# A decoder block in split fp32 on one core: SBUF pools in another order, so that weights start at a multiple of 128 bytes and the other large tiles 64 bytes past one

## The chip, the core and the metric

One core of a Trainium2 chip. The metric is device time in microseconds, from the start to the end of one execution. Two things beside it come from the profile of one execution: its span (first to last recorded instruction), and the start and duration of every instruction on the engines TensorE (PE; its weight loads are listed apart as PEld), VectorE (DVE), ScalarE (ACT), GpSimd (POOL) and of the DMAs that SyncE (SP) and GpSimd issue.

## The reference

One decoder layer on x of 512 tokens by 2048 channels, in float32:

```
h = rmsnorm(x);  proj = h @ w_in            # 2048 x 5132, three head groups
mixed = concat(pool_mixer, gated_deltanet, rglru_mixer)
x = x + mixed @ w_out                       # 2048 x 2048
up = rmsnorm(x) @ w_up                      # 2048 x 12288: gate and value, 6144 each
x = x + (gelu(causal_dwconv(gate)) * val) @ w_down   # 6144 x 2048
return rmsnorm(x)
```

Nearly all arithmetic is in the four products with w_in, w_out, w_up and w_down. The gated DeltaNet has six heads of 128 channels, with small 128 x 128 products between.

## The kernel before, in words

Every large float32 product is made from parts: an operand is split into `hi`, its value rounded to the type fp32r, and `lo`, the rest, and a product is three matmuls that add into one PSUM bank, hi·a, hi·b and lo·a (`mm3`, lines 199 to 203; L1187 in the up-projection). Each matmul has a 128 x 128 block of weights as its stationary operand, which a weight load brings in just before, and streams 512 or 256 columns of activations past it. Weights come by DMA as `raw` tiles of 4096 bytes a partition (three buffers); ScalarE casts one to `hi` and VectorE makes `lo` (four buffers each). These eleven buffers are the pool `wts`.

There are five stages, one behind the other on TensorE, whose order is written out by hand, as SyncE's is:

1. **f and u** (L329 to L371): 40 units of 128 columns of w_in, each over 16 blocks of 128 channels. The activations `xh`, `xl` lie in the pool `acts` (32 tiles of 2048 bytes a partition), 512 columns to a matmul. The first two units (outputs `ps_f`) run beside a small product `psab`; the other 38 (`ps_u`) have the small products of the DeltaNet heads between them, placed by coroutines with due times (`step`, `spawn`).
2. **o** (L390 and L888, outputs `ps_o`): 16 units of w_out with `yh`, `yl`, again in `acts`, 512 columns.
3. **up** (class `UpProjection`): each of 48 blocks j of w_up is made by a Strassen-like scheme from seven half products instead of eight. A half product is 8 blocks of channels by three matmuls with 256 columns, 24 matmuls in all (`product`, L1183 to L1190). The seven activation forms are a11 (tile `fa`), a12 and a22 (`fb`), and the four sums s1 to s4 (`fs`). `fa` and `fb` lie in `acts` (L846, L851). `fs` lies in the pool `ffn` for the first six of the eight blocks of channels (L827, tags `ea`) and in `acts` for the last two (L834). The forms of the seven are in `ACT_FORM` (L1125). The weight sums are made by DMA: after a block has been split, GpSimd issues a DMA that adds the next one to the same raw tile (L1172); a chain has up to three such steps, four slots apart, and the split runs three slots (`LAG`) ahead of its product. A slot is one half product.
4. **down** (L986 to L1007, outputs `ps_d`): 48 blocks of w_down, 512 columns; the activations `gs` lie in `ffn` (tags `r1` and `ea`, L957). VectorE adds each bank to an accumulator.
5. **the tail** (L1014 to L1114, outputs `ps_e`): the last two blocks of w_down in two halves of 256 columns, again from `gs`, with the final norm behind each half (`finish`).

SBUF is handed out by pools. A pool holds a buffer for each tag (times its `bufs`), in steps of 32 bytes a partition, and pools that are open together lie one behind another in the order in which they are opened (`run`, `in_phase` for stages 1 and part of 2, `out_phase` for the rest). The first one starts at a multiple of 128. So the place of a tile within 128 bytes follows from the sizes of the pools ahead of its own. In this text the place is the start address modulo 128. All large tiles are multiples of 128 bytes, so a pool of them hands its own place on; only small tiles shift it.

Of the kernel before, what the change touches and what calls it, by code (L numbers as in the profile page):

```python
# [8 lines left out]
F32 = mybir.dt.float32  # L9
# [9 lines left out]
P = 128  # L19
# [3 lines left out]
NC = S // P  # L23
# [17 lines left out]
NPRM = _o  # L41
# [38 lines left out]
class Body:  # L80
# [163 lines left out]
    def run(self):  # L244
        tc, nc, io = self.tc, self.nc, self.io
        with ExitStack() as ctx:
            pool = lambda name, **k: ctx.enter_context(tc.tile_pool(name=name, **k))
            self.cp = cp = pool("const", bufs=1)
            self.sm = pool("small", bufs=1)
            self.wp = pool("wts", bufs=1)  # L250
            self.ap_ = pool("acts", bufs=1)
            self.mm = pool("mm", bufs=4, space=PSUM)
            self.aux = pool("aux", bufs=4, space=PSUM)
            self.dr = pool("scratch", bufs=1, space=DRAM)
            ctx.enter_context(tc.manual_schedule(engines=MANUAL))
            self.prmt = cp.tile([P, NPRM], F32, name="prmt")
            cst = cp.tile([P, 4, P], F32, name="cst")
            self.ident, self.upper, self.mask, self.ones = (cst[:, i, :] for i in range(4))
            self.cst = cst
            self.in_phase()  # L260
            self.out_phase()
# [15 lines left out]
    def in_phase(self):  # L277
        tc, nc, io = self.tc, self.nc, self.io
        with ExitStack() as ctx:
            pool = lambda name, **k: ctx.enter_context(tc.tile_pool(name=name, **k))  # L280
            self.yp = pool("y", bufs=1)
            g1 = self.g1 = pool("g1", bufs=1)
            self.gp = pool("gp", bufs=1)
            self.tp = pool("tp", bufs=1)
            self.hd = {h: {} for h in range(H)}
            self.pr = {p: {} for p in range(H // 2)}
            self.lh, self.y = {}, {}
# [4 lines left out]
            wts = {0: [], 1: []}  # L292
# [36 lines left out]
            for kt in range(KT):  # L329
                if kt + 2 < KT:  # L330
                    x_tile(kt + 2)
                if kt == 4:
                    wts[0].append(self.prep_half(io["w_in"][0], 1, "in0"))
                    wts[1].append(self.prep_half(io["w_in"][1], 1, "in1"))
                if kt == 12:
                    nc.sync.dma_start(out=self.cst, in_=io["cst"])
                    nc.sync.dma_start(out=self.prmt, in_=io["prm"])
                for t, a in enumerate((ah, al)):
                    nc.tensor.matmul(psab, wab2[kt // 8][:, kt % 8, :], a[kt], start=kt == 0 and t == 0,
                                     stop=kt == KT - 1 and t == 1)  # L340
                sl = slice((kt % 8) * P, (kt % 8) * P + P)
                for u in range(2):
                    hi, lo = wts[u][kt // 8]
                    self.mm3(first[u], hi, lo, sl, ah[kt], al[kt], kt == 0, kt == KT - 1)
                self.step(8 * T_R)
# [13 lines left out]
            for n in range(2, NU):  # L359
# [7 lines left out]
                if n == NU - 3:  # L367
                    for b in range(NB):
                        self.ensure(lambda: 10 + b in self.y)
                        t = self.gp.tile([P, S], F32, tag=("kbT", "qT")[b % 2], name=f"yr{b}", bufs=(4, 3)[b % 2])  # L370
# [108 lines left out]
    def gdn_front(self, kind, h, ps):  # L479
        nc, gp = self.nc, self.gp  # L480
# [8 lines left out]
        if kind == "v":  # L489
            t = self.tmp(f"vT{h}")  # L490
# [13 lines left out]
            hd["bv"] = bv  # L504
            return
        sq = self.tmp(f"sq_{kind}{h}", [P, NC, P])
        ss = gp.tile([P, NC], F32, tag=f"ss_{kind}", name=f"ss_{kind}{h}", bufs=2)
        for c in range(NC):
            nc.scalar.activation(sq[:, c, :], tok[:, c, :], AF.Square, accum_out=ss[:, c:c + 1])
        nc.vector.tensor_scalar(ss, ss, EPS, None, op0=ALU.add)  # L510
        r = gp.tile([P, NC], F32, tag=f"r_{kind}", name=f"r_{kind}{h}", bufs=4)
        self.rsqrt(r, ss, f"r_{kind}{h}", NC)
        if kind == "q":
            nc.vector.tensor_scalar(r, r, float(P) ** -0.5, None, op0=ALU.mult)
# [7 lines left out]
            hd["at"] = at  # L522
            return

        br = gp.tile([P, NC], F32, tag="br", name=f"br{h}", bufs=2)
        nc.vector.tensor_tensor(out=br, in0=r, in1=self.beta[:, :, h], op=ALU.mult)
        kb = self.tmp(f"kb{h}", [P, NC, P])
        nc.vector.tensor_tensor(out=kb, in0=tok, in1=bc(br, P), op=ALU.mult)
        dr = gp.tile([P, NC], F32, tag="dr", name=f"dr{h}", bufs=2)
        nc.vector.tensor_tensor(out=dr, in0=r, in1=self.eD[:, :, h], op=ALU.mult)  # L530
        kd = gp.tile([P, NC - 1, P], F32, tag="kd", name=f"kd{h}", bufs=4)
        nc.vector.tensor_tensor(out=kd, in0=tok[:, 0:NC - 1, :], in1=bc(dr[:, 0:NC - 1], P), op=ALU.mult)
# [94 lines left out]
    def gdn_scan(self, h):  # L627
        nc, gp = self.nc, self.gp
        hd = self.hd[h]
        yield from self.wait(lambda: all(k in hd for k in ("TT", "at", "bv")))  # L630
        TT, at, kbT, bv, kd, qT = hd["TT"], hd["at"], hd["kbT"], hd["bv"], hd["kd"], hd["q"]
        o = self.tmp(f"o{h}", [P, NC, P])
        mo = gp.tile([P, NC], F32, tag="mo", name=f"mo{h}", bufs=2)
        sq = self.tmp(f"sqo{h}", [P, NC, P])
        st = None
        small = lambda tag, nm: self.tp.tile([P, P], F32, tag=tag, name=nm, bufs=3 if tag == "st" else 2)
        for c in range(NC):
            if c == 0:
                r = bv[:, 0, :]
            else:  # L640
                a = self.auxt(f"ps_s{h}_{c}")
                self.mm_s(a[:, 0, :], kbT[:, c, :], st)
                self.mm_s(a[:, 1, :], qT[:, c * P:(c + 1) * P], st)
                r = small("r", f"r{h}_{c}")
                nc.vector.scalar_tensor_tensor(out=r, in0=a[:, 0, :], scalar=self.neG[:, c, h:h + 1], in1=bv[:, c, :],
                                               op0=ALU.mult, op1=ALU.add)
                o1 = small("o1", f"o1{h}_{c}")
                nc.scalar.activation(o1, a[:, 1, :], AF.Copy, scale=self.eG[:, c, h:h + 1])
                yield Y1
            b = self.auxt(f"ps_v{h}_{c}")  # L650
            self.mm_s(b[:, 0, :], TT[:, c, :], r)
            vn = small("vn", f"vn{h}_{c}")
            nc.scalar.copy(out=vn, in_=b[:, 0, :])
            yield Y2
            if c < NC - 1:
                d = self.auxt(f"ps_d{h}_{c}")
                self.mm_s(d[:, 0, :], kd[:, c, :], vn)
                st2 = small("st", f"st{h}_{c}")
                if c == 0:
                    nc.vector.tensor_copy(st2, d[:, 0, :])  # L660
                else:
                    nc.vector.scalar_tensor_tensor(out=st2, in0=st, scalar=self.eGl[:, c, h:h + 1], in1=d[:, 0, :],
                                                   op0=ALU.mult, op1=ALU.add)
                st = st2
            po = self.auxt(f"ps_o{h}_{c}")
            self.mm_s(po[:, 0, :], at[:, c, :], vn)
            if c == 0:
                nc.vector.tensor_copy(o[:, 0, :], po[:, 0, :])
            else:
                nc.vector.tensor_tensor(out=o[:, c, :], in0=po[:, 0, :], in1=o1, op=ALU.add)  # L670
            nc.scalar.activation(sq[:, c, :], o[:, c, :], AF.Square, accum_out=mo[:, c:c + 1])
            yield Y3
        rq = hd["rq"]
        t = gp.tile([P, NC], F32, tag="mo2", name=f"mo2{h}", bufs=2)
        nc.vector.scalar_tensor_tensor(out=t, in0=rq, scalar=1.0 / P, in1=rq, op0=ALU.mult, op1=ALU.mult)
        nc.vector.tensor_tensor(out=mo, in0=mo, in1=t, op=ALU.mult)
        nc.vector.tensor_scalar(mo, mo, EPS, None, op0=ALU.add)
        fac = gp.tile([P, NC], F32, tag="fac", name=f"fac{h}", bufs=2)
        self.rsqrt(fac, mo, f"ro{h}", NC)
        nc.vector.tensor_tensor(out=fac, in0=fac, in1=rq, op=ALU.mult)  # L680
        nc.gpsimd.tensor_tensor(out=o, in0=o, in1=bc(fac, P), op=ALU.mult)
        yield 11.0
        pt = self.auxt(f"ps_ot{h}")
        for c in range(NC):
            self.tr_s(pt[:, c, :], o[:, c, :])
        yt = self.yp.tile([P, S], F32, name=f"y_gdn{h}")
        nc.scalar.activation(yt, pt.rearrange("p c d -> p (c d)"), AF.Copy, scale=self.prm("gnw"))
        hd["o"] = yt
# [96 lines left out]
    def out_phase(self):  # L785
        tc, nc, io = self.tc, self.nc, self.io
        with ExitStack() as ctx:
            pool = lambda name, **k: ctx.enter_context(tc.tile_pool(name=name, **k))
            g2 = pool("g2", bufs=1)
            ep = self.ep = pool("ffn", bufs=1)  # L790


            xp = []
# [191 lines left out]
            n = 0  # L985
# [50 lines left out]
            def finish(t, late):  # L1036
# [4 lines left out]
                n = HS // P  # L1041
                sums(t, late[-2:] + [s3[:, t, :]], last=True)
                pt = pts[t]
                ms = g2.tile([P, n], F32, tag=f"ms{n}", name=f"ms3_{t}", bufs=2)
                nc.vector.tensor_scalar(ms, pt[:, 0:n], 1.0 / D, EPS, op0=ALU.mult, op1=ALU.add)
                rt = g2.tile([P, n], F32, tag=f"rt{n}", name=f"rt3_{t}", bufs=2)
                self.rsqrt(rt, ms, f"n3_{t}", n)
                yield 3.0
                ps = self.aux.tile([P, S], F32, tag="aux", name=f"n3_ps{t}")
# [259 lines left out]
```

## Time and profile before

| | us |
|---|---|
| median of 3 runs | 2253.5 |
| lowest and highest | 2253.31, 2254.08 |
| the profiled execution, its time | 2254.35 |
| its span | 2252.6 |

The rest of the time, 1.75 us, lies around the span. The granted TensorE clock was 0.993 of full over the span. TensorE is recorded as busy for 2215.5 us, VectorE for 1520.4, ScalarE for 943.9 and GpSimd for 437.9. Matmuls overlap in the records: each one's duration holds a latency that the next one does not wait for. The pace of the work is therefore the distance from one start to the next, which a timeline, or the first and the last start of a group with its count, gives.

### The profile page before, as it was taken

The numbers are of one execution on the slowest core, as the hardware profiler recorded it, in microseconds if no ns is written. First come the engines' busy times: TensorE is split into PE (matmuls) and PEld (weight loads), VectorE is DVE, ScalarE is ACT, GpSimd is POOL, SyncE is SP. The second block draws the span as 40 slices with busy tenths as digits, with TensorE's granted clock in tenths as the row PEclk, the third lists the DMA queues.
The fourth block names the chain that finished last, engine by engine and source line by source line (L and its number), as shares of the span: only waits on it lengthen the run. The fifth ranks groups of instructions, "written<-read, shape, count | busy, mean of one in ns | idle before, by whom it ended". The sixth has DMA issues, their size and how long they took to land.

```text
span 2252.6 us, 35469 instructions
## 1 busy us (share of the span) xinstructions
PE 2215.5 (98%) x13998; PEld 1990.0 (88%) x13998; DVE 1520.4 (67%) x2340; ACT 943.9 (42%) x1371; POOL 437.9 (19%) x531
## 2 busy tenths in 40 slices
PE   9999999999999999999999999999999999999997
PEld 6878878888888999999999999999997888888886
DVE  8756657665545767666676766667667777777776
ACT  6646455434334544444444444444442222222223
POOL 4370731810122111111111111111110000000004
PEclk9999999999999999999999999999999999999998
DMA  6231222223534788888888888888875333333333
GB/s 197 82 98 62 87 87 84 88 89 113 187 126 136 152 201 204 206 201 202 200 204 192 202 205 200 204 202 201 210 188 187 112 122 112 122 113 122 113 123 102
DMA packets 109208, 340.01 MB, mean 151 GB/s; under 512 B 12720, under 2 KB 19120, under 8 KB 109040
## 3 DMA queue, kind: packets, MB, share of 16 engines
q1 hardware_dynamic: 78576, 229.72, 29.8%
q0 software_dynamic: 30464, 108.02, 26.3%
q8 instruction: 110, 1.80, 0.3%
q14 instruction: 58, 0.48, 0.1%
HBM read 314.36 MB, written 23.33 MB: 150 GB/s over the span
## 4 chain that ended last, share of the span: by engine, by line
PE 88%; POOL 4%; DVE 3%; issue 2%; ACT 1%; DMA 1%; SPq 0%; POOLq 0%; ACTq 0%; DVEq 0%
PE ps_y L1187 18%; PE ps_x L1187 12%; PE ps_z L1187 12%; PE ps_d L201 8%; PE ps_d L202 8%; PE ps_d L203 8%; PE ps_u L201 4%; PE ps_u L202 4%; PE ps_u L203 4%; PE ps_o L203 3%; PE ps_o L202 3%; PE ps_o L201 3%; POOL tm L581 2%; POOL tl L583 2%; PE ps_yt L118 1%
## 5 line engine op out<-in xcount | busy, mean ns | idle before, releaser
L1007 DVE TENSOR_TENSOR accd<-accd,ps_d 128x512 f32<-128x512 f32 x368 | 252.0, 686 | 138.6 <-PE ps_d L203 137.6
L201 PE MATMUL ps_d<-gs,whi_d 128*128 128x512 f32 x736 | 290.0, 394 | 0.0
L202 PE MATMUL ps_d<-gs,whi_d 128*128 128x512 f32 x736 | 290.0, 394 | 0.0
L203 PE MATMUL ps_d<-gs,wlo_d 128*128 128x512 f32 x736 | 290.0, 394 | 0.0
L1187 PE MATMUL ps_y<-fs,hi_t 128*128 128x256 f32 x1536 | 269.7, 278 | 1.1 <-DVE e L1213 1.1
L274 ACT CAST whi_d<-raw_d 128x1024 fp32r<-128x1024 f32 x96 | 100.5, 1051 | 388.0 <-PE ps_d L202 366.4
L1169 DVE TENSOR_TENSOR lo_t<-ra,hi_t 128x1024 fp32r<-128x1024 f32 x144 | 176.2, 1223 | 112.5 <-ACT hi_t L1168 112.4
L201 PE MATMUL ps_u<-xh,hi_in 128*128 128x512 f32 x608 | 246.3, 405 | 0.0
L203 PE MATMUL ps_u<-xh,lo_in 128*128 128x512 f32 x608 | 238.5, 392 | 0.0
L202 PE MATMUL ps_u<-xl,hi_in 128*128 128x512 f32 x608 | 237.9, 391 | 0.0
L1172 POOL DMA_DIRECT2D ra<-in_w_up x144 | 126.2, 876 | 557.5 <-DVE lo_t L1169 456.1
L1187 PEld LDWEIGHTS ps_y<-fs,hi_t 128*128 128x128 f32 x1536 | 232.9, 188 | 1.3 <-ACT h L1230 1.3
L1187 PE MATMUL ps_y<-fs,lo_t 128*128 128x256 f32 x768 | 213.1, 277 | 0.0
L1168 ACT CAST hi_t<-ra 128x1024 fp32r<-128x1024 f32 x144 | 151.5, 1052 | 74.4 <-PE ps_y L1187 46.1
L203 PEld LDWEIGHTS ps_d<-gs,wlo_d 128*128 128x128 f32 x736 | 137.6, 187 | 34.2
L201 PEld LDWEIGHTS ps_d<-gs,whi_d 128*128 128x128 f32 x736 | 137.6, 187 | 34.1
L202 PEld LDWEIGHTS ps_d<-gs,whi_d 128*128 128x128 f32 x736 | 137.6, 187 | 33.9
L189 DVE TENSOR_TENSOR lo_in<-raw_in,hi_in 128x1024 fp32r<-128x1024 f32 x80 | 104.4, 1307 | 78.0 <-ACT hi_in L188 77.4
L1187 PEld LDWEIGHTS ps_y<-fs,lo_t 128*128 128x128 f32 x768 | 144.3, 188 | 0.0
L1187 PE MATMUL ps_x<-fb,hi_b 128*128 128x256 f32 x768 | 141.4, 285 | 0.0
L1187 PE MATMUL ps_y<-fb,hi_t 128*128 128x256 f32 x768 | 140.1, 283 | 1.3 <-DVE e L1217 1.3
L1187 PE MATMUL ps_x<-fa,hi_b 128*128 128x256 f32 x768 | 140.0, 283 | 0.0
(357 smaller groups left out, 5109.4 us busy)
## 6 DMA issues: line engine op xcount, KB each, us to landing
ra<-in_w_up POOLq DMA_DIRECT2D x144, 512.0 KB, 7.8
raw_d<-in_w_down SPq DMA_DIRECT2D x96, 512.0 KB, 4.2
raw_in<-in_w_in SPq DMA_DIRECT2D x80, 512.0 KB, 3.7
ra<-in_w_up SPq DMA_DIRECT2D x48, 512.0 KB, 7.0
rc<-in_w_up SPq DMA_DIRECT2D x48, 512.0 KB, 6.5
rb<-in_w_up SPq DMA_DIRECT2D x48, 512.0 KB, 7.3
rb<-in_w_up POOLq DMA_DIRECT2D x48, 512.0 KB, 7.3
raw_o<-in_w_out SPq DMA_DIRECT2D x32, 512.0 KB, 3.8
```

The costliest lines, as they stand in the source:

```text
L189: nc.vector.tensor_tensor(out=lo, in0=raw, in1=hi.bitcast(F32), op=ALU.subtract)
L201: nc.tensor.matmul(ps, hi[:, sl], a, start=start, stop=False)
L202: nc.tensor.matmul(ps, hi[:, sl], b, start=False, stop=False)
L203: nc.tensor.matmul(ps, lo[:, sl], a, start=False, stop=stop)
L274: self.nc.scalar.copy(out=hi, in_=x)
L581: nc.gpsimd.tensor_tensor(out=t, in0=bc(ll[:, j, j + 1:32], j + 1), in1=tl[:, j:j + 1, 0:j + 1].broadcast_to([32, m, j + 1]), op=ALU.mult)
L583: nc.gpsimd.tensor_tensor(out=tl[:, j + 1:32, 0:j + 1], in0=tl[:, j + 1:32, 0:j + 1], in1=t, op=ALU.subtract)
L1007: nc.vector.tensor_tensor(out=acc[d], in0=acc[d], in1=ps, op=ALU.add)
L1168: nc.scalar.copy(out=hi, in_=raw)
L1169: nc.vector.tensor_tensor(out=lo, in0=raw, in1=hi.bitcast(F32), op=ALU.subtract)
L1172: nc.gpsimd.dma_start(out=raw, in_=self.block(j, self.NEXT[f]), accum_op=ALU.add)
L1187: mm = lambda w, x, s, e: nc.tensor.matmul(ps, w[:, sl], x, start=s, stop=e, skip_group_check=True)
```

## The change

Nothing that is computed changes, and no loop. The pools are opened in another order, and the small tiles get pools of their own, so that other start addresses come out:

- `wts` is opened first, ahead of `const` and `small`; in `const` the four constant blocks stand first and the parameter tile is 24 columns wider (the DMA still fills 305 of its columns).
- The small tiles of the heads (`ss`, `r`, `br`, `dr`, `mo`, `mo2`, `fac`; 16 bytes a partition each) leave `gp` for a new pool `gs`, and `g1` is opened after it, behind `tp`.
- In `out_phase`, `ffn` is opened ahead of `g2`.
- The two small tiles `ms2` and `rt2` of the final norm have one buffer instead of two.

```diff
         with ExitStack() as ctx:
             pool = lambda name, **k: ctx.enter_context(tc.tile_pool(name=name, **k))
+
+            self.wp = pool("wts", bufs=1)
             self.cp = cp = pool("const", bufs=1)
             self.sm = pool("small", bufs=1)
-            self.wp = pool("wts", bufs=1)
             self.ap_ = pool("acts", bufs=1)
...
-            self.prmt = cp.tile([P, NPRM], F32, name="prmt")
             cst = cp.tile([P, 4, P], F32, name="cst")
+            self.prmt = cp.tile([P, NPRM + 24], F32, name="prmt")
...
             self.yp = pool("y", bufs=1)
-            g1 = self.g1 = pool("g1", bufs=1)
             self.gp = pool("gp", bufs=1)
             self.tp = pool("tp", bufs=1)
+            self.gs = pool("gs", bufs=1)
+            g1 = self.g1 = pool("g1", bufs=1)
...
-                    nc.sync.dma_start(out=self.prmt, in_=io["prm"])
+                    nc.sync.dma_start(out=self.prmt[:, 0:NPRM], in_=io["prm"])
...
-        ss = gp.tile([P, NC], F32, tag=f"ss_{kind}", name=f"ss_{kind}{h}", bufs=2)
+        ss = self.gs.tile([P, NC], F32, tag=f"ss_{kind}", name=f"ss_{kind}{h}", bufs=2)
...
+            ep = self.ep = pool("ffn", bufs=1)
             g2 = pool("g2", bufs=1)
-            ep = self.ep = pool("ffn", bufs=1)
...
-                ms = g2.tile([P, n], F32, tag=f"ms{n}", name=f"ms3_{t}", bufs=2)
+                ms = g2.tile([P, n], F32, tag=f"ms{n}", name=f"ms3_{t}", bufs=1)
...
-                rt = g2.tile([P, n], F32, tag=f"rt{n}", name=f"rt3_{t}", bufs=2)
+                rt = g2.tile([P, n], F32, tag=f"rt{n}", name=f"rt3_{t}", bufs=1)
```

The tiles `r`, `br`, `dr`, `mo`, `mo2` and `fac` change from `gp` to `self.gs` in the same way as `ss`.

More of the change, by code (lines that the diff above doesn't have):

```diff
@@ L510, in gdn_front @@
         nc.vector.tensor_scalar(ss, ss, EPS, None, op0=ALU.add)
-        r = gp.tile([P, NC], F32, tag=f"r_{kind}", name=f"r_{kind}{h}", bufs=4)
+        r = self.gs.tile([P, NC], F32, tag=f"r_{kind}", name=f"r_{kind}{h}", bufs=4)
         self.rsqrt(r, ss, f"r_{kind}{h}", NC)
@@ L523, in gdn_front @@
             return
-        br = gp.tile([P, NC], F32, tag="br", name=f"br{h}", bufs=2)
+        br = self.gs.tile([P, NC], F32, tag="br", name=f"br{h}", bufs=2)
         nc.vector.tensor_tensor(out=br, in0=r, in1=self.beta[:, :, h], op=ALU.mult)
@@ L528, in gdn_front @@
         nc.vector.tensor_tensor(out=kb, in0=tok, in1=bc(br, P), op=ALU.mult)
-        dr = gp.tile([P, NC], F32, tag="dr", name=f"dr{h}", bufs=2)
+        dr = self.gs.tile([P, NC], F32, tag="dr", name=f"dr{h}", bufs=2)
         nc.vector.tensor_tensor(out=dr, in0=r, in1=self.eD[:, :, h], op=ALU.mult)
@@ L632, in gdn_scan @@
         o = self.tmp(f"o{h}", [P, NC, P])
-        mo = gp.tile([P, NC], F32, tag="mo", name=f"mo{h}", bufs=2)
+        mo = self.gs.tile([P, NC], F32, tag="mo", name=f"mo{h}", bufs=2)
         sq = self.tmp(f"sqo{h}", [P, NC, P])
@@ L673, in gdn_scan @@
         rq = hd["rq"]
-        t = gp.tile([P, NC], F32, tag="mo2", name=f"mo2{h}", bufs=2)
+        t = self.gs.tile([P, NC], F32, tag="mo2", name=f"mo2{h}", bufs=2)
         nc.vector.scalar_tensor_tensor(out=t, in0=rq, scalar=1.0 / P, in1=rq, op0=ALU.mult, op1=ALU.mult)
@@ L677, in gdn_scan @@
         nc.vector.tensor_scalar(mo, mo, EPS, None, op0=ALU.add)
-        fac = gp.tile([P, NC], F32, tag="fac", name=f"fac{h}", bufs=2)
+        fac = self.gs.tile([P, NC], F32, tag="fac", name=f"fac{h}", bufs=2)
         self.rsqrt(fac, mo, f"ro{h}", NC)
```

## The prediction

> **What bounds the kernel now.** I read the page first, then the busy time by stage.
>
> ```profile
> span 2252.6 us, 35469 instructions
> ...
> PE 88%; POOL 4%; DVE 3%; issue 2%; ACT 1%; DMA 1%; SPq 0%; POOLq 0%; ACTq 0%; DVEq 0%
> ```
>
> ```profile
> 40.00:565.00 525.00, 511.68 (x2567) 430.84 (x2566) 333.70 (x779) 257.94 (x471) 186.00 (x253) 0.99 0.28 90
> 565.00:745.00 180.00, 180.00 (x813) 149.79 (x812) 90.04 (x113) 68.78 (x90) 33.83 (x32) 1.00 0.46 149
> 745.00:1690.00 945.00, 941.22 (x8021) 940.75 (x8020) 658.55 (x826) 450.38 (x582) 165.45 (x189) 1.00 0.85 199
> 1690.00:2215.00 525.00, 523.74 (x2282) 421.35 (x2282) 382.98 (x525) 125.71 (x148) 0.82 (x2) 1.00 0.38 124
> 2215.00:2253.00 38.00, 23.64 (x194) 22.57 (x192) 23.02 (x70) 15.52 (x42) 23.69 (x33) 0.81 0.34 111
> ```
>
> The second answer's columns are window, length, busy time of PE, PEld, DVE, ACT and POOL, clock, DMA share, GB/s. The chain of waits is TensorE for 88%, and from u to down (rows 1 to 4) TensorE has work all the time, at full clock. So the time is the number of matmuls times the distance between their starts, and the question is whether that distance hangs on where the operands lie. The timeline of the up stage, for two half products, says that it may (start, duration, ..., xcount):
>
> ```profile
> 900.29 0.28 PE L1187 MATMUL ps_x<-fb,lo_b 128*128 128x256 f32 x1
> ...
> 901.37 0.28 PE L1187 MATMUL ps_x<-fb,lo_b 128*128 128x256 f32 x1
> ```
>
> ```profile
> 902.08 0.28 PE L1187 MATMUL ps_y<-fs,lo_t 128*128 128x256 f32 x1
> ...
> 903.78 0.28 PE L1187 MATMUL ps_y<-fs,lo_t 128*128 128x256 f32 x1
> ```
>
> Nine matmuls lie from start to start in the first (three to each `lo`): 1.08/9 = 0.120 us each. Fifteen in the second: 1.70/15 = 0.1133. Shape, weight pool and clock are the same; the activations are not in the same pool. The same holds of whole half products in the chain:
>
> ```profile
> 789.10 2.88 PE ps_y L1187 x24
> ...
> 907.18 2.88 PE ps_y L1187 x24
> 910.05 2.77 PE ps_z L1187 x24
> ...
> 1674.70 2.88 PE ps_y L1187 x24
> ```
>
> 2.88/24 is 0.120 again (`fb`, all in `acts`), while 2.77 is 18 at 0.1133 from `ffn` and 6 at 0.120 from `acts` (2.04 + 0.72 = 2.76). With 512 columns it goes the other way (count, min/median/max ns, first and last start):
>
> ```profile
> L201 PE MATMUL ps_o<-yh,hi_o x256: 389/389/389, 566.6 to 740.0; 128*128 128x512 f32 x128
> ```
>
> ```profile
> L201 PE MATMUL ps_d<-gs,whi_d x736: 394/394/402, 1694.3 to 2208.8; 128*128 128x512 f32 x184
> ```
>
> Each is every third matmul: o is (740.0 - 566.6)/255/3 = 0.2267 us (`acts`), down (2208.8 - 1694.3)/735/3 = 0.2333 (`ffn`).
>
> **The places.** They follow from the code: a tile takes a multiple of 32 bytes, the pools lie one behind another, the first at a multiple of 128. Before: `const` is 1220 (takes 1248) + 2048 = 3296 = 25·128 + 96, `small` 12·32 = 384, so `wts` is at place 96; it is 11·4096 long, so `acts` is at 96 too. `g2` behind it has 4096 + 6·32 = 4288 bytes, which puts `ffn` at 32. So weights and `acts` lie 0 apart, weights and `ffn` 64 apart. After: `wts` is at 0; `const`, 2048 + 1344 = 3392 = 26·128 + 64, puts `small`, `acts` and behind it `y`, `gp`, `tp` and `ffn` all at 64. Everything of size is then 64 from the weights. My reading is that the weight load of the next matmul and the columns of the current one meet in SBUF, and that the difference of their places decides how often:
>
> - 256 columns: 0.120 at 0 apart, 0.1133 at 64 apart
> - 512 columns: 0.2267 at 0 apart, 0.2333 at 64 apart
>
> That it is the difference and not a peculiarity of `fs` or `gs` is borne out by the tail, whose `gs` and weights lie as in down, with 256 columns:
>
> ```profile
> L1187 PE MATMUL ps_y<-fs,hi_t 128*128 128x256 f32 x1536 | 269.7, 278 | 1.1 <-DVE e L1213 1.1
> ...
> L1187 PE MATMUL ps_x<-fa,hi_b 128*128 128x256 f32 x768 | 140.0, 283 | 0.0
> ...
> L202 PE MATMUL ps_e<-gs,whi_d 128*128 128x256 f32 x64 | 17.7, 277 | 0.0
> ```
>
> A recorded duration is the distance plus a latency of about 163 ns (283 for 120, 389 for 226.7, 161 for down). `ps_e` at 277 is on the fast side with `fs`, though its tiles are those that are slow at 512 columns.
>
> **Up, gains.** The two quoted rows at 789.10 and 1674.70 are 45 blocks apart: 885.60/45 = 19.68 us a block. With all 168 matmuls at 0.1133, a block takes 19.04. 48 blocks times 0.64 are **-30.7 us**, if nothing else holds the stage. What might is the chain of weight sums: split, add by DMA, split again.
>
> ```profile
> L1169 DVE TENSOR_TENSOR lo_t<-ra,hi_t 128x1024 fp32r<-128x1024 f32 x144 | 176.2, 1223 | 112.5 <-ACT hi_t L1168 112.4
> L1168 ACT CAST hi_t<-ra 128x1024 fp32r<-128x1024 f32 x144 | 151.5, 1052 | 74.4 <-PE ps_y L1187 46.1 <-DMA ra<-in_w_up 24.2 <-PE ps_z L1187 4.2
> L1172 POOL DMA_DIRECT2D ra<-in_w_up x144 | 126.2, 876 | 557.5 <-DVE lo_t L1169 456.1
> ...
> ra<-in_w_up POOLq DMA_DIRECT2D x144, 512.0 KB, 7.8
> ```
>
> One step is 1.05 + 1.22 + 0.88 + 7.8 = 10.95 us. Four slots are 4/7·19.68 = 11.25 now and 10.88 after. A chain of three steps falls back by 3·0.07 = 0.2 us and then starts anew from a plain load, against a split that runs three slots (8.2 us) ahead. That covers it. Without the cover, the block would be 7/4·10.95 = 19.16 and the gain 25 us instead of 30.7. The DMA engines' share rises from 0.85 to 0.85·19.68/19.04 = 0.88, and VectorE's from 0.70 to 0.72: neither becomes the bound.
>
> **u and o, loss.** Both read `acts` with 512 columns and go from 0 to 64 apart. o: 768 matmuls times 6.67 ns, **+5.1 us**. u is less regular, since small products break its sequence:
>
> ```profile
> L201 PE MATMUL ps_u<-xh,hi_in 128*128 128x512 f32 x608 | 246.3, 405 | 0.0
> L203 PE MATMUL ps_u<-xh,lo_in 128*128 128x512 f32 x608 | 238.5, 392 | 0.0
> L202 PE MATMUL ps_u<-xl,hi_in 128*128 128x512 f32 x608 | 237.9, 391 | 0.0
> ```
>
> L202 and L203 lie 2 to 3 ns above o's 389 (L201's 405 holds waits), so u runs at about 0.2292 now and would lose 4.1 ns times 1824: **+7.5**. The bounds are 0 (if its broken sequences cost the same at any place) and 1824·6.67 = 12.2. The 96 matmuls of `ps_f` add at most 0.6.
>
> **Down and tail, nothing.** 64 apart before and after. Down stays at 0.2333.
>
> **The small products** of the heads pair `gp` (64 before) with `tp` (0 before), which become 0 apart.
>
> ```profile
> L118 PE MATMUL ps_x<-T,LT 128*128 128x128 f32 x96 | 11.8, 276 | 2.4 <-DMA T<-d 2.4
> ...
> L118 PE MATMUL ps_o<-vn,at 128*128 128x128 f32 x48 | 9.3, 279 | 0.0
> ```
>
> `T` and `LT` are both in `gp`, `vn` and `at` in `tp` and `gp`: 3 ns apart, on some 300 records, within 1 us either way. I take 0.
>
> **Other engines.** VectorE's places matter as little: with all operands in `ffn` 690 ns, with one from `g2`, 64 apart, 685. They are off the path anyway.
>
> ```profile
> L275 DVE TENSOR_TENSOR gs<-graw,gs 128x512 fp32r<-128x512 f32 x48 | 33.1, 690 | 0.0
> ...
> L1226 DVE TENSOR_TENSOR h<-gv,rstd 128x512 f32<-128x512 f32 x48 | 32.9, 685 | 0.0
> ```
>
> **Waits that the new layout could add.** The single buffers of `ms2` and `rt2` make the second half's `ms` wait for the first half's readers, the matmuls that spread `rt` over the columns, whose copy (L1052) VectorE already waits for here:
>
> ```profile
> 2232.21 0.48 DVE L1060 SCALAR_TENSOR_TENSOR accd<-accd,prmt,n_ps 128x256 f32<-128x256 f32 x1 [0.74 <-ACT rstd L1052]
> ...
> 2238.42 0.15 DVE L1045 TENSOR_SCALAR ms<-ps_n 128x2 f32<-128x2 f32 x1
> ```
>
> They are over 6 us before the second `ms`: nothing. In `out_phase` the tiles of `ffn` now lie over other tiles of the first phase. The residual's loads, issued on SyncE's queue with w_out's next weights behind them, wait for the last `y` to be split; now the third load is the one that does, before it was the second. The queue is held until the same moment: nothing.
>
> **Sum.** -30.7 + 5.1 + 7.5 = -18.1. The profiled execution's own 2254.35 becomes 2236.25; the median of the runs shown is 0.85 below that execution, so **2235.4**.
>
> **Rivals.** *Better at 512 columns too.* Both operands also move from 32 bytes off a 64-byte boundary onto one, which no steady stage of the trace shows together with weights. If down then runs at 0.2267, and u and o keep theirs, 2208·6.67 ns = 14.7 come on top of 30.7: 2253.5 - 45.4 = 2208. [...] Against: nothing shows that the 32 bytes count.
>
> *Slower.* The same move turns out the other way: at the new places the up stage's `fs` run at the slow pace too. Then 48·4·18 = 3456 matmuls lose 6.67 ns (+23.0), `fa` and `fb` gain nothing, and u and o lose their 12.6: 2289. It decides from the half product `ps_z` on: 2.88 instead of 2.72. Against it: the differences of places above explain every stage without it.
>
> *Nothing changes.* The two paces belong to the tiles and the order of work in a stage. Then 0.120 and 0.1133, 0.2267 and 0.2333 stay where they are: 2253.5. Against it stands `ps_e`. [...]
>
> *The weight chain binds*, as priced above: 25 instead of 30.7, 2241.
>
> **Chances.** The forecast 0.50, the weight chain 0.08, better 0.18, nothing 0.11, slower 0.13. Faster by over 0.2% (4.5 us, about what a measurement of this kernel can tell from no change) is 0.76, within 0.11, slower 0.13. The range leaves out the slower rival and a little on the other side: from 2205 (the better rival with 3 us for the unknown of u) to 2254. The forecast's own range is 2230 to 2242 (u's bounds, the chain).
>
> **What would show it.** In the profile after, every half product of up is 2.72 long in the chain; a block takes 19.04; `ps_o` and `ps_u` record 394 to 396 ns instead of 389; `ps_d` stays at 394; TensorE stays busy throughout up. It would be wrong if `fa`'s 283 stays, if `ps_d` moves, or if TensorE starts to wait for `lo` tiles.

## The result and the profile after

The changed kernel took 2266.71 us (median of 4 runs, 2264.28 to 2268.16), the kernel before, on the same chip, 2253.40 (2253.29 to 2254.08): a ratio of 1.0057, with a 95% interval of 1.004 to 1.0075. It is slower by some 13 us; forecast were 18 us less. The profiled execution took 2264.28 us, 9.9 more than that of before, and all the differences below are of these two. Of the runs further down, one execution of e2 (3122 us, at a granted clock of 0.653) and one of e10 (4863 us) are left out. The page of after, its span and its chain of waits:

```profile
span 2262.5 us, 35469 instructions
...
PE 86%; POOL 5%; DVE 3%; issue 2%; DMA 1%; ACT 1%; SPq 0%; POOLq 0%; ACTq 0%; DVEq 0%
```

TensorE is the bound as before. The busy time by stage, in the same columns as before's:

```profile
40.00:565.00 525.00, 517.33 (x2562) 428.37 (x2561) 333.99 (x780) 256.55 (x468) 184.38 (x253) 1.00 0.29 90
565.00:745.00 180.00, 180.00 (x773) 144.23 (x773) 86.91 (x107) 67.39 (x89) 31.46 (x29) 1.00 0.44 143
745.00:1690.00 945.00, 942.01 (x7993) 941.17 (x7992) 654.14 (x822) 446.08 (x577) 167.07 (x192) 1.00 0.85 199
1690.00:2215.00 525.00, 522.37 (x2289) 422.84 (x2288) 381.90 (x522) 128.84 (x149) 0.00 (x0) 1.00 0.39 126
```

TensorE still has work all the time in up (942.0 of 945 us), and the granted clock there is 1.00. In row 2 the same 180 us hold 773 matmuls where they held 813; 37 of these 40 are the first ones of up, which now starts behind the window. By the start of each stage's first matmul, the 9.9 us are spread so:

| stage | before, us | after, us | difference | forecast |
|---|---|---|---|---|
| until u | 42.7 | 43.2 | +0.5 | 0 |
| u, with the heads' small products | 523.9 | 524.9 | +1.0 | +7.5 |
| o | 174.0 | 179.2 | +5.2 | +5.1 |
| up | 953.7 | 957.0 | +3.3 | -30.7 |
| down | 515.2 | 515.2 | 0 | 0 |
| tail | 43.1 | 43.0 | -0.1 | 0 |

Nearly all that is wrong lies in up. The chain of waits of after there (start, length, tile, line, matmuls):

```profile
1632.67 2.83 PE ps_x L1189 x24
1635.49 2.83 PE ps_y L1189 x24
1638.32 2.83 PE ps_x L1189 x24
1641.14 0.04 issue
1641.18 2.98 PE ps_y L1189 x24
1644.16 2.72 PE ps_z L1189 x24
1646.88 2.72 PE ps_y L1189 x24
```

This is the most telling place of the trace. Up to 1641 us, but for the first few, a half product takes 2.83 us, whether it reads `fs`, `fa` or `fb`: 0.1178 a matmul, which no stage of before had. From there on it takes 2.72, the forecast's 0.1133, to the end of the stage. In between TensorE paused once, by some 0.2 us; tiles, shapes and places are the same on both sides. The timeline of TensorE shows the pause:

```profile
1639.45 0.28 PE L1189 MATMUL ps_x<-fb,lo_b 128*128 128x256 f32 x1
...
1640.87 0.28 PE L1189 MATMUL ps_x<-fb,lo_b 128*128 128x256 f32 x1
1641.18 0.47 PE L1189 MATMUL ps_y<-fs,hi_t 128*128 128x256 f32 x2
1641.50 0.28 PE L1189 MATMUL ps_y<-fs,lo_t 128*128 128x256 f32 x1
...
1642.86 0.28 PE L1189 MATMUL ps_y<-fs,lo_t 128*128 128x256 f32 x1
```

From the first `lo_b` to the second lie twelve starts, 1.42/12 = 0.118 us; from `lo_t` to `lo_t` twelve more, 1.36/12 = 0.113. One layout has two steady paces; they are called steps from here on. From start to start, 309 of the 336 half products ran at 117.8 ns and 21 at 113.3; the rest hold waits. A block took 19.787 us for nearly the whole stage, against 19.680 before and 19.04 forecast.

The other stages, by tile (count, min/median/max ns, first and last start), for o and down:

```profile
L201 PE MATMUL ps_o<-yh,hi_o x256: 394/394/394, 568.1 to 746.6; 128*128 128x512 f32 x128
```

```profile
L201 PE MATMUL ps_d<-gs,whi_d x736: 388/396/398, 1704.3 to 2218.8; 128*128 128x512 f32 x184
```

o is at (746.6 - 568.1)/255/3 = 0.2333, as forecast. Down keeps 0.2333 on average ((2218.8 - 1704.3)/735/3), though its single records now spread from 388 to 398. u goes to 0.2334 between neighbours too, and yet its stage is only 1.0 us longer. The waits of TensorE from 0 to 565 us (us in total, times, longest) say why; before, and then after:

```profile
PE ps_yt L118 <- ACT hi_in L188: 5.7, 1, 5.7
PE tok_v L122 <- ACT vT L494: 4.4, 2, 3.2
PE ps_x L118 <- DMA T<-d: 2.4, 2, 1.2
```

```profile
PE ps_yt L118 <- ACT hi_in L188: 4.1, 1, 4.1
...
PE tok_v L122 <- ACT vT L496: 1.7, 2, 1.3
...
PE ps_x L118 <- DMA T<-d: 0.9, 1, 0.9
```

TensorE waits there for other engines at a few places, 12.5 us in these rows. With slower matmuls it arrives later and waits 6.7.

### The profile page after: what moved, and what is told of

Its sections match the earlier page's. It is cut to its first block, busy times and chain, and to the rows that moved or that the text cites. A ratio compares the mean times of both kernels' runs of the same rounds, so it can differ in the third digit from the quotient of the medians.

```text
span 2262.5 us, 35469 instructions
## 1 busy us (share of the span) xinstructions
PE 2230.0 (99%) x13998; PEld 1992.6 (88%) x13998; DVE 1520.8 (67%) x2340; ACT 943.8 (42%) x1371; POOL 434.6 (19%) x531
## 4 chain that ended last, share of the span: by engine, by line
PE 86%; POOL 5%; DVE 3%; issue 2%; DMA 1%; ACT 1%; SPq 0%; POOLq 0%; ACTq 0%; DVEq 0%
PE ps_y L1189 17%; PE ps_x L1189 12%; PE ps_z L1189 12%; PE ps_d L202 8%; PE ps_d L203 8%; PE ps_d L201 8%; PE ps_u L201 4%; PE ps_u L202 4%; PE ps_u L203 3%; PE ps_o L203 3%; PE ps_o L202 3%; PE ps_o L201 3%; POOL tl L585 2%; POOL tm L583 2%; PE ps_yt L118 1%
## 5 line engine op out<-in xcount | busy, mean ns | idle before, releaser
L1189 PE MATMUL ps_y<-fs,hi_t 128*128 128x256 f32 x1536 | 275.3, 281 | 1.4 <-DVE e L1215 1.4
L203 PEld LDWEIGHTS ps_u<-xh,lo_in 128*128 128x128 f32 x608 | 114.1, 188 | 27.8
```

The source lines that it names most:

```text
L203: nc.tensor.matmul(ps, lo[:, sl], a, start=False, stop=stop)
L1189: mm = lambda w, x, s, e: nc.tensor.matmul(ps, w[:, sl], x, start=s, stop=e, skip_group_check=True)
```

## The experiments

The theory after the result: the pace hangs on the distance of columns and weights, but in up there is something more that chooses between two steps. The rivals: the places themselves count (32 bytes off a 64-byte boundary); another order of the pools brings a new wait; the step is chance, whatever the layout.

Distances are given as columns' start less weights' start. They follow from the sizes: `wts` takes 45056 bytes, 176 times 256, and before `acts` stood right behind it; `acts` (65536) and `g2` (4288 = 16·256 + 192) put `ffn` 192 past a multiple of 256. After, `const` and `small` lie between (3392 + 384 = 14·256 + 192).

**e1, before, all 32 bytes further.**

```diff
-            self.prmt = cp.tile([P, NPRM], F32, name="prmt")
+            self.prmt = cp.tile([P, NPRM + 8], F32, name="prmt")
...
```

> The kernel before with every tile 32 bytes further on: weights and acts at place 0, ffn at 64. All distances between weights and activations are those of before, only the 64-byte boundary is met. If the distance alone sets the pace, all stages keep theirs: 2253. If starts on a boundary are what made the up stage slow in the changed kernel, its fs run at 0.1178 us instead of 0.1133 also here: 48 blocks times 72 matmuls times 4.5 ns, +15.5, so 2269. If the pace is a matter of how the stream happens to be in step after its last interruption, fs lie between 0.1133 and 0.1178 and differ from half product to half product.

2253.96 us (2252.67 to 2256.48, 10 runs), ratio 0.9998 (0.9989 to 1.0008). Its chain keeps before's two lengths:

```profile
904.40 2.76 PE ps_z L1187 x24
907.16 2.88 PE ps_y L1187 x24
```

Weights and `acts` now stand on a 64-byte boundary, and nothing moves. So the boundary is not what made up slow, and with it falls the ground of the prediction's "slower" and "better" rivals, the move onto a boundary.

**e2 and e3, after's order with the weights at 96.** The parameter tile gets a pool ahead of `wts`. In e2 a pad of 64 bytes in `const` keeps all else 192 past the weights; e3 has no pad, which gives 128.

```diff
+            self.prmt = pool("prm", bufs=1).tile([P, NPRM], F32, name="prmt")
             self.wp = pool("wts", bufs=1)
...
-            cst = cp.tile([P, 4, P], F32, name="cst")
-            self.prmt = cp.tile([P, NPRM + 24], F32, name="prmt")
+            cst = cp.tile([P, 4 * P + 16], F32, name="cst")[:, 0:4 * P].rearrange("p (a b) -> p a b", a=4)
...
```

> The order of pools of the changed kernel, but weights at 96 and all other large tiles at 32: 64 apart everywhere, as in the changed kernel, and off the 64-byte boundary, as fs and weights were before. If the boundary is what the forecast missed, up runs at 0.1133 throughout and the forecast's sum holds: 2235. If it is the step that the stream falls into after an interruption, up keeps one pace for long stretches, 0.1133 or 0.1178, and the time lies between 2235 and 2267. u, o and down at 0.2333 in either case.

> Weights and all other large tiles at 96: 0 apart everywhere, off the boundary. By the distance: u and o at 0.2267 as before, down at 0.2267 instead of 0.2333 (2208 times 6.67 ns, -14.7), all of up at 0.120 (3456 matmuls of fs lose 6.67 ns, +23.0): 2262. If down stays at 0.2333, its pace belongs to the stage and not to the place, and the time is 2276.

e2: median 2266.95 us, ratio 1.0014 (0.997 to 1.0058). Its runs are of two kinds: seven lie from 2265.26 to 2268.91, two at 2233.72 and 2233.91. The profiled one is of the long kind, with half products of 2.83:

```profile
906.67 2.83 PE ps_y L1189 x24
```

The two kinds are some 33 us apart, and 44 blocks of 19.787 - 19.04 = 0.747 are 33: the short kind has the time that the fast step through nearly all of up would give, though no trace of one was taken. So this layout, with after's distances, has two times, and the forecast's 2235 is close to the shorter. After's own four runs all lay at the longer one.

e3: 2271.1 us (2270.05 to 2272.03), ratio 1.0071 (1.0056 to 1.0086), neither of the two times expected. By the prediction's rule (places mod 128) it is 0 apart like before's `acts`, so that o should have run at 226.7. It did not:

```profile
L201 PE MATMUL ps_o<-yh,hi_o x256: 390/393/405, 566.9 to 744.7; 128*128 128x512 f32 x128
```

(744.7 - 566.9)/255/3 = 0.2324. A distance of 128 isn't one of 0.

**e4, the paces alone.** A kernel whose TensorE has matmuls only, 144 at each of sixteen distances; the trace is of its one execution:

```python
for d in order:                        # distance 8 * d columns, 32 * d bytes
    for n, nm in ((512, "full"), (256, "half")):
        ...
                    o = 8 * d + 512 * ((2 * j + h) % 6)
                    nc.tensor.matmul(ps[:, 0:n], w[:, c:c + P], m[:, o:o + n], ...)
```

> Nothing of the reference is computed: only TensorE runs, the sequence hi times a, hi times b, lo times a over eight weight blocks, 144 matmuls for each of sixteen distances of columns from weights (0 to 480 bytes in steps of 32, tiles named by a letter a to p), with 512 and with 256 columns, the whole twice in two orders. Theory 1, only the distance modulo 128 counts: four paces that come back every 128 bytes, at 64 bytes 0.1133 or 0.1178 us with 256 columns and 0.2333 with 512, at 0 bytes 0.2267 and 0.120. Theory 2, the pattern is longer, 256 bytes: the up and o stages of the kernel before were at 0 of 256 (0.120, 0.2267) and its fs and down at 192 (0.1133, 0.2333), the last run at 128 (0.1187, 0.2324), and 64 of 256 has not been seen; a, c, e and g then differ and come back at i, k, m and o. Theory 3, the pace belongs to the step into which the stream falls: the two passes differ at the same distance.

Its rows by tile; a is a distance of 0, c 64, g 192, i 256, k 320, o 448:

```profile
L115 PE MATMUL ps_half_c<-m,w x144: 276/276/276, 153.2 to 169.4; 128*128 128x256 f32 x144
...
L115 PE MATMUL ps_full_g<-m,w x144: 393/397/399, 321.8 to 355.1; 128*128 128x512 f32 x144
L115 PE MATMUL ps_half_g<-m,w x144: 280/281/281, 355.4 to 372.2; 128*128 128x256 f32 x144
...
L115 PE MATMUL ps_full_i<-m,w x144: 389/389/395, 423.0 to 455.4; 128*128 128x512 f32 x144
L115 PE MATMUL ps_half_i<-m,w x144: 278/283/283, 455.6 to 472.8; 128*128 128x256 f32 x144
```

The second pass, in another order, at 64 and at 192:

```profile
L115 PE MATMUL ps_half_c_again<-m,w x144: 279/279/283, 1010.6 to 1027.4; 128*128 128x256 f32 x144
```

```profile
L115 PE MATMUL ps_half_g_again<-m,w x144: 276/276/283, 1212.9 to 1229.1; 128*128 128x256 f32 x144
```

Last less first start, over 143, is the pace: at 256 it is 0.2266 and 0.1203, the same as at 0, and the paces of 64 and of 192 also come back 256 bytes on (first pass: 0.2287 at 64 and at 320, 0.2329 and 0.1175 at 192 and at 448). For 512 columns 0 is best (226.7 ns), 64 takes 228.9, the others 232.4 to 234.3. For 256 columns 0 and 96 are worst (120.0), 32, 128, 160 and 224 take 116.7 to 118.7, and 64 and 192 have two values: 64 took 113.3 in the first pass and 192 took 117.5 by the row (117.78 between neighbours); in the second 64 took 117.5 by the row and 192 took 113.3. So there are two steps, at one distance and in one shape, with nothing on TensorE but matmuls, and what came ahead may choose. The two passes differ at some other distances as well, by less: 32 took 116.7 and then 117.8, 160 took 117.4 and then 118.7, and 128 with 512 columns 233.4 and then 232.4.

So the distance of the two operands counts: at one shape and a granted clock of 1.00, before has 226.7 ns in o and 233.3 in down, and 120.0 and 113.3 in up. That the load of the weights and the columns meet in SBUF was the author's reading in the prediction; whether the two reads are what meets, no run shows.

**e5, what chooses the step.** Eight half products of 24 matmuls, at 64 (near) or 192 (far), after leads of 24 to 27 matmuls; then the same with the last three of each at distance 0 ("three"), then plain again ("then"). Again the trace is of one execution.

> Nothing of the reference is computed: eight half products of 24 matmuls with 256 columns in a row, at distance 64 (near) or 192 (far), after a lead of 24 to 27 matmuls with 512 columns (a to d), first plain, then with the last three matmuls of each half product at distance 0, then plain again; at the end once with the last six. If the pace at 64 and 192 belongs to the step that the stream is in, plain is 0.1133 after some leads and 0.1178 after others. If a stretch at distance 0 sets the step, as the fs of the kernel before suggest (their last six matmuls of 24 were at 0, and they came back to 0.1133 every time), then every run is at 0.1133 again after it: 'three' costs some 0.03 us a half product over 24 times 0.1133, and 'then' is 0.1133 after every lead. If it doesn't, 'then' has the pace of 'plain'.

```profile
L108 PE MATMUL ps_far_plain_a<-m,w x192: 280/281/281, 105.0 to 127.5; 128*128 128x256 f32 x192
L108 PE MATMUL ps_far_three_a<-m,w x192: 274/276/287, 127.6 to 149.5; 128*128 128x256 f32 x192
L108 PE MATMUL ps_far_then_a<-m,w x192: 276/276/282, 149.6 to 171.3; 128*128 128x256 f32 x192
L108 PE MATMUL ps_near_plain_b<-m,w x192: 276/276/276, 177.1 to 198.8; 128*128 128x256 f32 x192
...
L108 PE MATMUL ps_near_then_b<-m,w x192: 279/279/283, 221.5 to 244.0; 128*128 128x256 f32 x192
```

Far: (127.5 - 105.0)/191 = 0.1178 plain, and 21.7/191 = 0.1136 after the stretch with distance 0. Near: 0.1136 plain, 0.1178 after it. The plain runs fell into either step, by the lead; the "then" runs were at 113.4 after all four leads for far and at 117.8 after all four for near. So a few matmuls at distance 0 put a stream at 192 into its fast step, as expected, and one at 64 into its slow step, against the expectation (0.1133 after every lead). This fits the kernel before: there `fs` at 192 always ran among `fa` and `fb` at 0.

**e6, before with `ffn` at 64 instead of 192.**

```diff
+            pad = pool("pad", bufs=1).tile([P, 16], F32, name="pad")
+            nc.gpsimd.memset(pad, 0.0)
+            ep = self.ep = pool("ffn", bufs=1)
             g2 = pool("g2", bufs=1)
-            ep = self.ep = pool("ffn", bufs=1)
...
```

> The kernel before with ffn alone moved, from 192 to 64 behind the weights (modulo 256), by opening it ahead of g2 behind 64 unused bytes. By the table of distances: down at 0.2289 instead of 0.2333 (2208 times 4.45 ns, -9.8), everything else as before if fs, which come out of a stretch at distance 0, go on at 0.1133: 2244. If they fall into 0.1178: 3456 times 4.45 ns more, 2259. If only the distance modulo 128 counts, nothing changes: 2254.

2270.15 us (2269.18 to 2271.99), ratio 1.0071 (1.0056 to 1.0086): neither of the two. The chain and down:

```profile
906.25 2.85 PE ps_z L1189 x24
909.09 2.88 PE ps_y L1189 x24
```

```profile
L201 PE MATMUL ps_d<-gs,whi_d x736: 397/397/400, 1709.7 to 2224.2; 128*128 128x512 f32 x184
```

`ps_z` goes from before's 2.77 to 2.85: 18 at 117.8 and 6 at 120.0 would be 2.84. Among matmuls at distance 0, a stream at 64 is in its slow step, as in e5. Down stays at (2224.2 - 1709.7)/735/3 = 0.2333 where 228.9 was expected.

**e7, everything 64 from the weights.** Without the 24 columns of padding, and with one buffer less in `small`.

```diff
-        t = self.sm.tile([P, n], F32, tag=f"rs_t{n}", name=f"{tag}_t", bufs=3)
+        t = self.sm.tile([P, n], F32, tag=f"rs_t{n}", name=f"{tag}_t", bufs=3 if n == NC else 2)
...
-            self.prmt = cp.tile([P, NPRM + 24], F32, name="prmt")
+            self.prmt = cp.tile([P, NPRM], F32, name="prmt")
```

> The changed kernel without the 24 columns of the parameter tile and with one small tile less, so that acts, ffn and the rest lie 64 bytes behind the weights modulo 256 instead of 192. By the table: down -9.8, o +1.7 and u about +1 against the kernel before, and up either at 0.1133 throughout (-30.7: 2216) or at 0.1178 (+5: 2252), as its step falls; runs of both kinds, and mixed ones, are possible. If 64 and 192 are the same, as the change takes them, it is 2267 like the changed kernel.

2252.24 us (2248.59 to 2254.23), ratio 0.999 (0.998 to 1.0), the second of the two times. Down:

```profile
L201 PE MATMUL ps_d<-gs,whi_d x736: 388/388/388, 1702.2 to 2206.9; 128*128 128x512 f32 x184
```

Down is at (2206.9 - 1702.2)/735/3 = 0.2289, o too, u at 229.2 ns; up stayed in the slow step throughout, 19.787 a block. At 64 instead of 192 the change would not have lost against before.

**e8, after with a kick**, that is, with a few matmuls of each block at distance 0. Two activation tiles, with kt = 7 of two of the four forms of `fs`, go into a pool right behind the weights, at distance 0.

```diff
             self.wp = pool("wts", bufs=1)
+            self.kp = pool("kick", bufs=1)
...
+    def act(self, tag):
+        return self.kp if tag in ("ah14", "al14") else self.ap_
...
```

> The changed kernel, with two of its activation tiles (2 KB each; they hold kt = 7 of the forms s2 and s4) laid right behind the weights, at distance 0 from them; all else stays at 192. Two of the seven half products of a block then end with three matmuls at distance 0. Theory (at 192 the stream of half products has two steady steps, 113.3 and 117.8 ns; a short stretch at distance 0 puts it in the fast one): a block of up takes 168 at 113.33 plus six times 6.67 ns = 19.08 us instead of 19.787; some 45 blocks give back 31.8 us, two of 32 tiles of u and o at distance 0 another 1: about 2234 us. Rival (which of the two steps holds is chance, decided at some wait of TensorE, and a few matmuls at another distance don't move it): blocks stay at 19.79 plus 0.04, and the time at 2266.

2234.9 us (2233.06 to 2236.3, 4 runs), ratio to before 0.9912 (0.9897 to 0.9927). In the chain, 2.72 is a half product in the fast step, and 2.73 one that ends in the kick or follows it:

```profile
903.50 2.73 PE ps_x L1195 x24
906.24 2.72 PE ps_y L1195 x24
908.96 2.72 PE ps_z L1195 x24
```

A block takes 19.080 us, as worked out. The stage falls out of the fast step twice in the trace (blocks of 19.28 and 19.60 near its start, 19.82 and 19.60 near its end) and comes back within two blocks, where after had stayed in the slow step for 44. Only two tiles of 2 KB lie at another distance than in after. So the order of the pools and the waits that it brings have no part in what up lost.

**e9, the kick from down's tiles.** The four tiles of `gs`, two of which hold `fs` of kt = 0 in up, go into a pool at distance 0. Five buffers of `small` and the padding of the parameter tile go, 256 bytes in all, which leaves the other distances at 192.

```diff
+            pad = pool("pad", bufs=1).tile([P, 16], F32, name="pad")
+            nc.gpsimd.memset(pad, 0.0)
+            self.zp = pool("gsp", bufs=1)
...
-                t = ep.tile([P, 2, S], F32R, tag=("r1", f"ea{i}")[odd], name=f"gs{j}", bufs=(2, 1)[odd])
+                t = self.zp.tile([P, 2, S], F32R, tag=("r1", f"ea{i}")[odd], name=f"gs{j}", bufs=(2, 1)[odd])
...
```

> The changed kernel, with weights, activations and most of ffn as there, 192 apart, but with the four 4 KB tiles that hold gs (down's columns) and, in up, fs of kt = 0 in a pool of their own at distance 0 from the weights. By the distances: down runs at 226.67 instead of 233.33 ns (2208 times 6.67 = -14.7 us; its tail with 256 columns loses about 1), and four half products of each block of up begin with three matmuls at distance 0, which hold the other matmuls in the fast step: a block is 168 at 113.33 plus twelve times 6.67 = 19.12 instead of 19.787, -30 us. Together 2222 to 2224. Rivals: only down gains (up stays in its slow step): 2253; nothing gains: 2267.

2222.15 us (2221.05 to 2222.62, 4 runs), ratio to before 0.9855 (0.9841 to 0.987). Chain and down:

```profile
905.84 2.74 PE ps_y L1192 x24
908.58 2.74 PE ps_z L1192 x24
911.32 2.72 PE ps_y L1192 x24
```

```profile
L201 PE MATMUL ps_d<-gs,whi_d x736: 389/389/392, 1676.7 to 2176.5; 128*128 128x512 f32 x184
```

2.74 is 21 at 113.3 and 3 at 120.0; a block takes 19.120. Down is at (2176.5 - 1676.7)/735/3 = 0.2267. Both gains come as worked out, and this version beats both kernels.

**e10, e7 with everything 32 bytes further.** It asks for the reason of e6's down.

```diff
+            lead = pool("lead", bufs=1).tile([P, 8], F32, name="lead")
             self.wp = pool("wts", bufs=1)
...
```

> The layout with weights, activations and ffn all 64 apart, with everything 32 bytes further on, so that weights lie at 160 and columns at 224 mod 256 (before: 128 and 192). It asks why down at 64 ran at 228.9 in that layout and at 233.3 where the kernel before had only its ffn moved to 64. If the distance alone counts: u, o and down at 228.9, up at 117.8, 2252 us. If at 64 it also counts whether a tile begins on a multiple of 64 bytes: down at 233.3, up near 118.6, some 2268 to 2275.

2252.39 us, ratio 0.9989 (0.9979 to 0.9999), with down as in e7 (row by tile), (2206.4 - 1701.7)/735/3 = 0.2289:

```profile
L201 PE MATMUL ps_d<-gs,whi_d x736: 394/394/397, 1701.7 to 2206.4; 128*128 128x512 f32 x184
```

The boundary is not the reason. 512 columns at 64 have two steady paces too: from neighbour to neighbour all of e6's down runs at 233 or 234 ns, while e7's and e10's go between 225 and 232. What put e6 there stays open; e4 shows only the faster one.

All layouts side by side (distances mod 256; paces from start to start):

| kernel | `acts` | `ffn` | block of up, us | o, ns | down, ns | time, us |
|---|---|---|---|---|---|---|
| before, e1 | 0 | 192 | 19.68 | 226.7 | 233.3 | 2253.4, 2254.0 |
| after | 192 | 192 | 19.79 | 233.3 | 233.3 | 2266.7 |
| e2 | 192 | 192 | 19.79 (profiled) | 233.3 | 233.3 | 2267.0 or 2233.8 |
| e3 | 128 | 128 | 19.94 | 232.4 | 232.4 | 2271.1 |
| e6 | 0 | 64 | 20.03 | 226.7 | 233.3 | 2270.2 |
| e7, e10 | 64 | 64 | 19.79 | 228.9 | 228.9 | 2252.2, 2252.4 |
| e8 | 192, two tiles 0 | 192 | 19.08 | 233.1 | 233.3 | 2234.9 |
| e9 | 192 | 192, four tiles 0 | 19.12 | 233.3 | 226.7 | 2222.2 |

## Why the prediction was wrong, point by point

**The step that failed** is "With all 168 matmuls at 0.1133, a block takes 19.04." The sum took 0.1133 as the pace of a distance. It is the pace of one of two steps at that distance, and before held it because a part of each block ran at distance 0. The change took that part away, to gain 6.67 ns on each of its matmuls; the stream then fell into the other step, 117.8, for 309 of up's 336 half products. At 48 blocks the two steps are 48·0.747 = 35.9 us apart, more than the forecast's gain; up came out at +3.3 instead of -30.7. e5 shows this alone (0.1178 plain, 0.1136 after a stretch at distance 0), e8 and e9 show it in the kernel (blocks of 19.08 and 19.12 us instead of 19.787). Which step a stream at 192 falls into when nothing in it lies at distance 0 is not settled by the distance: e2 had both.

**The evidence for it** was thinner than it looked. Every `fs` row of before stood among matmuls at distance 0. The one row without them, `ps_e` at 277, is 192 matmuls behind down's, and was read as a rule of the distance.

**Places mod 128** was wrong; the period is 256 (e3, e4). For this change it did no harm: before's 64 apart and after's 64 apart are both 192.

**u and o** were right in pace (233.4 and 233.3). o's +5.1 came as +5.2. Of u's +7.5 only +1.0 was left, because TensorE's waits for other engines in that stretch took up about 6 of it. The prediction named no such cover, though row 1 of its table by stage left 13.3 us idle in u.

**Down and tail, the small products, the new waits**: 0, as forecast; the only new wait of TensorE in the trace is one of 0.6 us in u (`ps_x`, for a tile of GpSimd). **The weight chain** did not bind: TensorE is busy 942.0 of 945 us in up, and e9's block took 19.12, less than the 19.16 at which that chain was priced.

**The rivals.** "Nothing changes" fell with u and o. "Slower" had the right sign, with another mechanism and a larger price (2289): e1 refutes its boundary, and `fs` went to 117.8, not 120.0. "Better at 512 columns too" fell with e1 and with down. The case that came true, one layout with two steady paces, was not among them, and the range ended at 2254. The forecast's own narrower range, 2230 to 2242, does not follow from the bounds given for it either: u at 0 alone gives 2227.9.

## What to carry to other kernels

In these runs, in which every fp32r matmul loads new weights, the distance of columns and weights in SBUF, mod 256 bytes, made up to 3% at 512 columns (226.7 to 234.3 ns) and 6% at 256 (113.3 to 120.0), for nothing but a few bytes of padding: a parameter to be measured like a tile size. A pace seen in a mixed stream belongs to the mixture; before all of it is moved to the "fast" place, measure that place by itself, several times and with different work ahead of it. And a stream with two steady steps may be held in the better one by a few matmuls at another distance: in e8 and e9 six and twelve of a block's 168, at 6.67 ns each, held it near 113.3 instead of 117.8.

## What was not expected of the hardware

- The pace of this case's fp32r matmuls, with a weight load each, has a period of 256 bytes in the distance of their operands: 226.7 ns at 0, 228.9 at 64 (233.3 in e6's down) and 232.4 to 234.3 elsewhere for 512 columns; 120.0 at 0 for 256 columns, 113.3 or 117.8 at 64 and 192.
- At 64 and 192 the two values are steady steps. After's trace stayed for 44 blocks (some 870 us) in one and left it at a pause of about 0.2 us. After a stretch with matmuls at distance 0, 192 is in the fast step (113.4 in e5) and 64 in the slow one (117.8). Why, the runs do not show.
- One program then has two times: e2's runs lay near 2267 or at 2233.8.
